# A hybrid decoder trunk on one core: the retention queries' projection ahead of the first gated-linear heads' projection

## The chip, the cores and the metric

The kernel runs on one core of a Trainium2 chip. The metric is the device time of one execution in microseconds (us). The engines that appear below are TensorE (PE, its weight load PEld), VectorE (DVE), ScalarE (ACT), GpSimd (POOL) and SyncE (SP, which issues the DMAs). Each runs its own instruction stream in order, and waits on semaphores of the others.

## The reference

There are two layers. Each is a half-step SwiGLU feed-forward block (FFN), a parallel mixing of tokens by three groups of heads, and a second half-step FFN; a final RMSNorm ends the trunk. There are 512 tokens, the model is 1024 wide and the FFN 2816, all in float32.

```python
for l in range(DEPTH):
    h = rms_norm(x, ffn1_norm[l])
    x = x + 0.5 * swiglu_ffn(h, ffn1_w_gate[l], ffn1_w_up[l], ffn1_w_down[l])
    h = rms_norm(x, mix_norm[l])
    (a_q, a_f, a_i, a_g, b_q, b_k, b_v, b_z, b_beta, b_a,
     c_q, c_k, c_v, c_g) = jnp.split(h @ w_in[l], SPLIT_IDX, axis=-1)
    o_a = hgrn2_mixer(a_q, a_f, a_i, a_g, lbs[l], hgrn_norm[l])
    o_b = gated_deltanet_mixer(b_q, b_k, b_v, b_z, b_beta, b_a, ...)
    o_c = retention_mixer(c_q, c_k, c_v, c_g, positions)
    mixed = jnp.concatenate([o_a, o_b, o_c], axis=-1)
    x = x + mixed @ w_out[l]
    h = rms_norm(x, ffn2_norm[l])
    x = x + 0.5 * swiglu_ffn(h, ffn2_w_gate[l], ffn2_w_up[l], ffn2_w_down[l])
return rms_norm(x, final_norm)
```

Each mixer has four heads. Group a is gated linear attention (HGRN2) with a decay per feature. Group b is the gated delta rule, which convolves q, k and v, and in each chunk of tokens solves a unit lower triangular system before it scans over the chunks. Group c is retention, which rotates q and k by the token's position (rope) and has a fixed decay per head.

## The kernel before, in words

**Dense products.** Every float32 operand of a dense product is split in two float32r parts, `hi` (a rounding on ScalarE) and `lo` (the remainder, on VectorE, or on GpSimd for every second split of a mixer: `POOL_LO`, `split`, line 199). A product is three matmuls. The FFNs are dense products alone (`mm3`, recorded as line 217).

**The mixer** (`mix`, line 1231) runs two things against each other. `dense_stream` (line 278) yields the matmuls of the input projection one at a time, in the order of `PLAN` (line 115), and then those of the output projection. The chains are Python generators that issue the work of the heads in steps. `interleave` (line 1308) takes a step of a chain when the chain is due by an estimate of the engines' time, and dense matmuls otherwise. A chain's step has a scheduling priority (`PRIO`: 4000 for b, 3000 for a and c, 500 for `pre`), and a limited number of chains runs at once (`LIMIT`, `CHAINS`).

A name in `PLAN` stands for one or more units of the input projection:

- `t0`: the retention values and the small gates of b. Tokens are on the partitions ("tm").
- `b0`, `b1`: q, k and v of the delta-rule heads 0, 1 and 2, 3. Features are on the partitions ("fm"); each of the three units has 256 columns, and each 128 of them are 24 matmuls of 512 columns. When a block is done, `b_conv` convolves it (tile `braw`), and after the last v `b_start` (line 599) and two `b_chain` (line 688) follow.
- `a0`, `a1`: f and q of the gated-linear heads 0, 1 and 2, 3, in "fm". `a_chain` (line 871) and `a_head` (line 912) follow.
- `ai`: the gated-linear values, in "tm".
- `cq`, `ck`: the retention queries and keys, in "tm", 256 columns: 96 matmuls of 256 columns. `c_rope` (line 1103) rotates each (tiles `craw`, `ctmp`, `crot`); when both are rotated two `c_pair` (line 1138) are queued (tiles `ps_kv`, `ps_cs`, `ps_co`).
- `bz0`, `bz1`, `cg`, `ag`: the output gates.

The triangular systems of a pair of b heads are inverted in `b_blocks` (line 638), a chain of small VectorE operations on the tiles `blk_s`, `blk_p`, `blk_x` and `inv`. The decays inside a chunk of a gated-linear head are built in levels: `aw` on VectorE, `ps_al` on TensorE, `a` back on VectorE. A `b_chain` ends in a scan over four chunks (`ps_scan`).

When all heads of a group and its gates are done, `out_group` normalises and gates it, and `flip_out` transposes and splits it (tiles `ps_mt`, `mh`, `ml`). The output projection adds the groups in three parts, `OUT_PARTS`: b0 with c, then b1, then a (matmuls `ps_out`). A part of `dense_stream` waits for its groups in this order, and the last part is in `out_proj`.

**Loads.** `stream_units` (line 230) walks the same plan. It issues one DMA of 1024 KB per 256 columns of an "fm" unit and two of 512 KB per "tm" unit on SP's queue, into two `raw` buffers, and each split goes to one of four `hi` and four `lo` buffers; `fetch` asks for the next while a unit is being multiplied.

Of the kernel before, what the change touches and what calls it, by code (L numbers as in the profile page):

```python
# [111 lines left out]
GROUP = {"a": 0, "b0": 1, "b1": 2, "c": 3}  # L112

OUT_PARTS = (('b0', 'c'), ('b1',), ('a',))
PLAN = 't0 b0 a0 ai cq b1 ck bz0 cg a1 ag bz1'

LIMIT = {'b': 4, 'a': 2, 'c': 2, 'pre': 9}
CHAINS = 6
# [47 lines left out]
class Kern:  # L166
# [1064 lines left out]
    def mix(self, l):  # L1231
# [12 lines left out]
        with self.pool(name="lay", bufs=1) as self.lay:  # L1244
# [54 lines left out]
            }  # L1299
            plan = [u for name in PLAN.split() for u in parts[name]]  # L1300
            self.units = self.stream_units(plan, self.io["w_out"][l])
# [223 lines left out]
```

## Time and profile before

| What | Value |
|---|---|
| Median of three runs | 2191.91 us (2185.59 to 2193.06) |
| Profiled execution | 2192.0 us, its span 2190.2 us |
| Mixer of layer 0, with the ends beside it | 375.6 to 753.4 us of the span |
| Mixer of layer 1, with the ends beside it | 1457.0 to 1834.2 us |
| Mean granted clock of TensorE | 0.992 |
| Bytes moved by DMA | 203.08 MB, mean 93 GB/s |

The span is the time between the first and the last instruction of the profile. A matmul's busy time overlaps that of the next one: one of 512 columns is shown with 0.39 us, while two of them start 0.23 us apart, so the distance between the starts is what one costs. The granted clock is 1.00 at full speed. A helper records most operations at one line (149 for VectorE, ScalarE and GpSimd, 260 and 265 for TensorE in the mixer), so groups are told apart by their tiles.

### The profile page before, as it was taken

How to read it: one execution, taken by the hardware profiler on the slowest of the kernel's cores; microseconds unless marked ns; L12 is line 12 of the kernel's file. 1: busy time of each engine (PE TensorE's matmuls, PEld its weight loads, DVE VectorE, ACT ScalarE, POOL GpSimd, SP SyncE). 2: the span in 40 equal slices, each digit the busy share in tenths (PEclk: the TensorE clock that was granted, in tenths of full speed). 3: DMA queues.
4: the chain of work that ended last, by engine and by line, in shares of the span. 5: the costliest groups of instructions: out<-in, count | busy, mean ns of one | idle time of the engine just before them, and what ended most of it. 6: DMA issues, size and time to landing. Idle time of an engine off the chain costs nothing.

```text
span 2190.2 us, 31776 instructions
## 1 busy us (share of the span) xinstructions
PE 2154.9 (98%) x13079; PEld 1829.6 (84%) x13079; DVE 1147.9 (52%) x1980; ACT 842.4 (38%) x1319; POOL 500.4 (23%) x466
## 2 busy tenths in 40 slices
PE   8999999998999999999999999999899999999998
PEld 7888888887988788888888888888889888888888
DVE  5544345468497743433543343364866876434335
ACT  5322224555555422222432222254654544222225
POOL 2201013454333210101211010133633412101011
PEclk9999999999999999999999999999999999999999
DMA  4323234221123323232232322242121232323223
GB/s 155 126 78 116 77 106 140 73 78 40 59 60 106 97 97 96 78 115 80 94 116 96 97 97 96 82 148 79 59 59 40 73 103 88 104 94 99 96 87 126
DMA packets 197757, 203.08 MB, mean 93 GB/s; under 512 B 7626, under 2 KB 189292, under 8 KB 197612
## 3 DMA queue, kind: packets, MB, share of 16 engines
q1 hardware_dynamic: 197612, 201.05, 29.0%
q8 instruction: 103, 1.69, 0.3%
q14 instruction: 42, 0.34, 0.0%
HBM read 194.74 MB, written 6.29 MB: 92 GB/s over the span
## 4 chain that ended last, share of the span: by engine, by line
PE 86%; DVE 9%; ACT 2%; issue 1%; POOL 0%; DMA 0%; SPq 0%; DVEq 0%; ACTq 0%; POOLq 0%
PE pd L217 22%; PE pu L217 22%; PE pg L217 22%; PE ps_fm L260 7%; PE ps_tm L260 5%; PE ps_out L260 2%; DVE aw L149 1%; PE ps_scan L265 1%; DVE lo L149 1%; PE ps_ss L265 1%; DVE blk_p L149 1%; DVE x L149 1%; PE ps_ao L265 1%; DVE flo L149 1%; PE ps_al L265 0%
## 5 line engine op out<-in xcount | busy, mean ns | idle before, releaser
L149 ACT CAST hi<-raw 128x1024 fp32r<-128x1024 f32 (+2 forms) x369 | 379.2, 1028 | 1094.2 <-PE pg L217 323.0
L149 DVE TENSOR_TENSOR lo<-raw,hi 128x1024 fp32r<-128x1024 f32 (+2 forms) x325 | 390.2, 1201 | 80.9 <-ACT hi L149 68.5
L149 POOL TENSOR_TENSOR g<-g,rstd 128x512 f32<-128x512 f32 x88 | 150.2, 1706 | 1130.2 <-ACT g L146 1130.2
L217 PE MATMUL pd<-ah,hi 128*128 128x512 f32 (+1 forms) x752 | 282.0, 375 | 0.0
L217 PE MATMUL pd<-ah,lo 128*128 128x512 f32 (+1 forms) x752 | 281.6, 375 | 0.0
L217 PE MATMUL pd<-al,hi 128*128 128x512 f32 (+1 forms) x752 | 281.6, 375 | 0.0
L217 PE MATMUL pg<-xl,hi 128*128 128x512 f32 x704 | 275.0, 391 | 1.0 <-DVE xl L149 1.0
L217 PE MATMUL pu<-xh,hi 128*128 128x512 f32 x704 | 274.4, 390 | 0.6 <-ACT hi L149 0.6
L217 PE MATMUL pg<-xh,hi 128*128 128x512 f32 x704 | 274.5, 390 | 0.1
L217 PE MATMUL pg<-xh,lo 128*128 128x512 f32 x704 | 274.2, 389 | 0.0
L217 PE MATMUL pu<-xh,lo 128*128 128x512 f32 x704 | 274.1, 389 | 0.0
L217 PE MATMUL pu<-xl,hi 128*128 128x512 f32 x704 | 273.9, 389 | 0.0
L149 DVE TENSOR_TENSOR u<-pu,g 128x512 f32<-128x512 f32 x88 | 60.9, 692 | 280.7 <-PE pu L217 265.2
L149 DVE SCALAR_TENSOR_TENSOR x<-pd,x 128x512 f32<-128x512 f32 (+1 forms) x104 | 67.4, 649 | 229.3 <-PE pd L217 229.0
L149 DVE TENSOR_TENSOR g<-pg,rstd 128x512 f32<-128x512 f32 x88 | 60.8, 691 | 206.8 <-PE pg L217 206.7
L217 PEld LDWEIGHTS pd<-al,hi 128*128 128x128 f32 x752 | 141.4, 188 | 25.7
L217 PEld LDWEIGHTS pd<-ah,lo 128*128 128x128 f32 x752 | 141.3, 188 | 25.4
L217 PEld LDWEIGHTS pd<-ah,hi 128*128 128x128 f32 x752 | 141.1, 188 | 25.5
L217 PEld LDWEIGHTS pg<-xl,hi 128*128 128x128 f32 x704 | 132.3, 188 | 29.3 <-DVE xl L149 2.1
L217 PEld LDWEIGHTS pg<-xh,hi 128*128 128x128 f32 x704 | 132.5, 188 | 27.8 <-ACT xh L149 0.4
L217 PEld LDWEIGHTS pu<-xh,hi 128*128 128x128 f32 x704 | 132.1, 188 | 28.2 <-ACT hi L149 1.0
L217 PEld LDWEIGHTS pu<-xh,lo 128*128 128x128 f32 x704 | 132.3, 188 | 27.5
(331 smaller groups left out, 3778.5 us busy)
## 6 DMA issues: line engine op xcount, KB each, us to landing
raw<-in_ffn_w_gate_dram SPq DMA_DIRECT2D x43, 1024.0 KB, 5.1
raw<-in_ffn_w_up_dram SPq DMA_DIRECT2D x43, 1024.0 KB, 5.1
raw<-in_ffn_w_down_dram SPq DMA_DIRECT2D x32, 1024.0 KB, 4.7
raw<-in_w_in_dram SPq DMA_DIRECT2D x20, 1024.0 KB, 5.2
raw<-in_w_in_dram SPq DMA_DIRECT2D x32, 512.0 KB, 3.6
raw<-in_ffn_w_down_dram SPq DMA_DIRECT2D x20, 768.0 KB, 4.4
xd<-x SPq DMA_DIRECT2D x16, 256.0 KB, 2.5
raw<-in_w_out_dram SPq DMA_DIRECT2D x16, 256.0 KB, 2.6
```

Of the source, the lines that this page charges most:

```text
L149: return f(*args, **kw)
L217: self.nc.tensor.matmul(ps, a[:, k, :], b, start=n == 0, stop=n == 3 * nk - 1)
L260: self.nc.tensor.matmul(ps, a, b, start=start, stop=stop)
L265: self.nc.tensor.matmul(ps, a, b, start=start, stop=stop)
```

## The change

The order of the units in `PLAN` changes. Nothing else does.

```diff
 OUT_PARTS = (('b0', 'c'), ('b1',), ('a',))
-PLAN = 't0 b0 a0 ai cq b1 ck bz0 cg a1 ag bz1'
+PLAN = 't0 b0 cq a0 ai ck b1 bz0 cg a1 ag bz1'
```

Two units move: `cq` from behind `ai` to ahead of `a0`, and `ck` from behind `b1` to ahead of it. So `a0` and `ai` have one more unit ahead of them, `b1` has one more, and from `bz0` on the same units stand in the same places. The loads and splits of the weights follow the same order. The chains are queued when their units are done, so their steps move with the units.

## The prediction

> **What bounds the kernel now.** I read the page first: the span, the engines and the weight loads of the mixers (count, KB each, us to landing).
>
> ```profile
> span 2190.2 us, 31776 instructions
> PE 2154.9 (98%) x13079; PEld 1829.6 (84%) x13079; DVE 1147.9 (52%) x1980; ACT 842.4 (38%) x1319; POOL 500.4 (23%) x466
> raw<-in_w_in_dram SPq DMA_DIRECT2D x20, 1024.0 KB, 5.2
> raw<-in_w_in_dram SPq DMA_DIRECT2D x32, 512.0 KB, 3.6
> ```
>
> TensorE is busy 98% of the span. An order of products removes none of them, so all that it can win is time in which TensorE idles or runs slowly, and all that it can lose is new time of that kind. The next view is the busy time by stretches: span of the stretch, then PE, PEld, DVE, ACT and POOL busy with instruction counts, then TensorE's granted clock, DMA share and GB/s. The first two rows are the mixers of layer 0 and 1 with their ends; the others are 15 us pieces.
>
> ```profile
> 375.60:753.40 377.80, 366.55 (x3316) 322.67 (x3315) 265.23 (x601) 200.12 (x375) 149.46 (x169) 0.98 0.24 72
> 1457.00:1834.20 377.20, 365.57 (x3316) 323.24 (x3315) 264.15 (x599) 201.01 (x375) 148.27 (x166) 0.98 0.24 73
> ...
> 480.00:495.00 15.00, 12.58 (x110) 9.92 (x109) 14.52 (x31) 7.67 (x12) 12.76 (x22) 0.89 0.13 36
> 495.00:510.00 15.00, 11.85 (x170) 9.49 (x169) 15.00 (x34) 6.17 (x16) 6.68 (x8) 0.89 0.13 36
> 510.00:525.00 15.00, 12.49 (x234) 9.54 (x235) 14.47 (x31) 6.42 (x9) 7.76 (x9) 0.89 0.13 37
> 660.00:675.00 15.00, 13.84 (x267) 12.33 (x266) 12.67 (x35) 10.78 (x25) 7.33 (x13) 1.00 0.45 135
> 675.00:690.00 15.00, 14.77 (x228) 12.34 (x227) 10.23 (x22) 8.21 (x21) 4.42 (x5) 1.00 0.32 115
> 1560.00:1575.00 15.00, 12.57 (x110) 10.03 (x110) 14.52 (x31) 7.80 (x12) 12.76 (x22) 0.89 0.12 35
> 1575.00:1590.00 15.00, 11.49 (x169) 9.39 (x168) 15.00 (x34) 6.16 (x16) 6.59 (x8) 0.89 0.14 38
> 1590.00:1605.00 15.00, 11.97 (x320) 9.76 (x318) 14.93 (x34) 6.42 (x10) 6.84 (x13) 0.95 0.14 37
> ```
>
> Each mixer leaves 377.80 - 366.55 = 11.2 and 377.20 - 365.57 = 11.6 us idle, and most of it sits in one place. In 480 to 525 TensorE is busy 36.9 of 45 us (8.1 idle), and the clock of 0.89 takes another 3 x 0.11 x 15 = 4.95: 13.0 us. In layer 1 the same 45 us have 9.0 idle and 4.0 of slow clock: 13.0 again. VectorE is full there (14.5, 15.0, 14.5 of 15). So **this stretch is bound by VectorE, and the rest of the mixer by TensorE**. The waits of TensorE in layer 0, and rows of the timeline of TensorE and of VectorE, say on what it waits (start, duration, engine, operation):
>
> ```profile
> PE ps_al L265 <- DVE a L149: 3.1, 1, 3.1
> PE ps_al L265 <- DVE ak L149: 2.4, 2, 2.1
> PE ps_fm L260 <- issue: 1.7, 1, 1.7
> ```
>
> ```profile
> 490.95 0.63 PE L260 MATMUL ps_fm<-xl,hi 128*128 128x512 f32 x1
> 517.92 0.73 PE L260 MATMUL ps_fm<-xh,hi 128*128 128x512 f32 x1 [1.70 <-issue]
> ```
>
> ```profile
> 466.94 1.58 DVE L149 TENSOR_TENSOR blk_s<-mt,cst 128x512 f32<-128x512 f32 x1
> 514.81 1.62 DVE L149 TENSOR_TENSOR inv<-blk_t,cst 128x128 f32<-128x128 f32 x2
> 516.69 1.21 DVE L149 TENSOR_TENSOR lo<-raw,hi 128x1024 fp32r<-128x1024 f32 x1
> 545.10 0.69 DVE L149 TENSOR_TENSOR braw<-ps_fm,rstd 128x512 f32<-128x512 f32 x1 [1.82 <-PE ps_fm L260]
> 593.84 0.91 DVE L149 TENSOR_TENSOR blk_s<-mt,cst 128x512 f32<-128x512 f32 x1
> 622.23 0.68 DVE L149 TENSOR_TENSOR inv<-blk_t,cst 128x128 f32<-128x128 f32 x2
> 706.17 1.40 DVE L149 SCALAR_TENSOR_TENSOR ml<-ps_mt,sv_a,mh 128x512 fp32r<-128x512 f32 x2
> 716.66 3.21 DVE L149 SCALAR_TENSOR_TENSOR o_a<-o_a,hr,g_a 128x64 f32<-128x64 f32 x16
> ```
>
> Three things queue on VectorE at once: the block inverses of the first delta-rule heads (b0: 466.94 to 516.4, 49.5 us, where b1's take 593.84 to 622.9, 29 us), the products of the first gated-linear heads (a0: the ps_al waits, in 480 to 525), and the rotation of the retention queries (cq). Even the dense stream waits: the weight remainder `lo` ends at 517.90 and TensorE starts at 517.92, the wait that the page calls issue.
>
> **The change part by part.** The dense order becomes t0, b0, cq, a0, ai, ck, b1, and from bz0 on it is as before. So cq stands ahead of a0 and ai, and ck ahead of b1, which the change's name doesn't say. The price of such a unit, by the chain of waits:
>
> ```profile
> 381.22 6.65 PE ps_tm L260 x54
> 398.46 19.73 PE ps_fm L260 x86
> ```
>
> 6.65 / 54 = 0.123 us per matmul, 96 of them: 11.8 us (a 512 wide product, second row, is 19.73 / 86 = 0.229). Then a0 comes 11.8 us later than now, b1 comes 11.8 us later, and ck earlier by all of b1's products and what lies between them. The loads move with their units on SP's queue: a unit of this kind brings two of 512 KB at 3.6 us each in 11.8 us of products, a feature unit one of 1024 KB at 5.2 us for 48 x 0.229 = 11.0; the DMA share stays below one half, so I put their cost at nothing. If that cover failed it would be some 5 us a layer, one landing.
>
> *VectorE's queue between 465 and 525.* cq's rotation leaves it (first row: what touches ctmp, DVE busy then POOL), and ck's comes in, from 560 to 585 (second row):
>
> ```profile
> 480.00:520.00 40.00, 5.28 (x8) 3.28 (x4) 0.89 0.12 31
> 560.00:585.00 25.00, 6.07 (x8) 2.59 (x3) 0.93 0.21 66
> ```
>
> That is an even exchange. What changes is a0: its work arrives 11.8 us later, so b0's inverses have VectorE nearly to themselves at first. If they run like b1's (29 us) they end near 496, where now they end at 516, and a0's levels, now in 480 to 525, come after them. Bounds for what is left of the 13.0 us: nothing better than the second gated-linear heads, which run the same levels without inverses beside them (660 to 690: 1.16 + 0.23 = 1.4 us idle, clock 1.00), and nothing worse than 13.0, as the same VectorE work then lies over a time 11.8 us longer. I take **5.0**: nearer the first, because the inverses go, and not at it, because ck's rotation stays beside a0. The gain is G = 8.0 us per layer.
>
> *b1's end.* b1's last convolution input is read at 545.10 and its mixed rows are ready at 706.17 + 1.40 = 707.6: 162.5 us, in steps. The end of the mixer is the next row (first product of the FFN), and the two output parts ahead of it, b1's and a's, are 96 products of 0.229 us, 22.0 us:
>
> ```profile
> 734.27 0.39 PE L217 MATMUL pg<-xh,hi 128*128 128x512 f32 x1
> ```
>
> So b1's part starts at 712.3 at the latest, 4.7 us after it is ready; a's transposes and waits come off that, and I take 2 us of slack (bounds 0 and 4.7). Group a's rows are done at 716.66 + 3.21 = 719.9, and its 48 products must start by 734.3 - 11.0 = 723.3. Both ends are nearly tight now. After the change b1's dense end moves by ck's 11.8, plus what else is pulled ahead of it, less G. Pulled ahead are the retention pairs, whose products take (ps_kv, ps_cs, ps_co in this order, PE first; DVE is the third figure):
>
> ```profile
> 560.00:612.00 52.00, 1.66 (x12) 1.50 (x12) 0.67 (x2) 0.63 (x2) 0.97 0.14 43
> 560.00:612.00 52.00, 3.50 (x32) 3.30 (x32) 2.54 (x4) 0.97 0.14 43
> 560.00:612.00 52.00, 5.23 (x44) 5.16 (x44) 1.41 (x4) 0.97 0.14 43
> ```
>
> Together 10.4 us. Now ck's unit can't end before 545.1 + 11.8 = 557, and the pairs lie between there and 612, at most 55 us behind. After the change it ends near 480 + 11.8 = 492, so the pairs come by 547, ahead of b1's end. An earlier b0 can also bring part of its scan ahead (first row below, up to 7.96 us from 545 to 570). Bounds: 11.8 - 8.0 = +3.8 with nothing pulled ahead, 11.8 + 10.4 + 8.0 - 8.0 = +22.2 with all. I take **+14.2**, the pairs alone. From there b1's steps lose company on VectorE: ck's rotation (6.07) and the pairs (0.67 + 2.54 + 1.41), 10.7 us. Bounds 0 and 10.7; I take all, as they are the whole difference in company there. b1 is ready 3.5 us later than now, while TensorE is at its part 8.0 earlier: a wait of 3.5 - 2 + 8.0 = 9.5 us. While TensorE has nothing else the steps of the scan need not share it:
>
> ```profile
> 545.00:570.00 25.00, 7.96 (x46) 6.33 (x46) 3.00 (x9) 3.66 (x10) 0.98 0.36 107
> ...
> 650.00:692.00 42.00, 11.24 (x68) 9.31 (x68) 3.62 (x12) 5.16 (x15) 1.00 0.36 115
> ```
>
> b1's scan has 11.24 + 3.62 + 5.16 = 20 us of work in 42 us, so half of the wait closes up: 4.8 us stays. Such a stop costs a slow stretch of clock as those at 480 to 525 did, 0.11 x 15 = 1.65 us. Behind the waiting product on TensorE stand a's part and the FFN, so all of it counts. Given back: 4.8 + 1.6 = 6.4 us.
>
> Trainium skill, "TensorE: Matmul & The Clock Gate", Part 1: a free-running window of about 3.4 us with too little activity halves the clock until a busy window has passed. By that figure a stop costs an estimated 1.7 us; the matmuls of 0.63 us in the first of the three pieces agree. It speaks against the change, which makes a long wait at the end out of several short ones.
>
> **Sum.** Per layer -8.0 + 6.4 = -1.6, twice: -3.2 us. The profiled execution took 2192.0 us (span 2190.2 and 1.8 around), the median of the three runs is 2191.91, so no correction: **2188.8 us**. A measurement of this kernel tells 0.3%, 6.6 us, from no change.
>
> **The rivals.** *Faster: b1 isn't late* (chance 0.35). If the pairs fall behind b1's end, b1's dense end moves by 3.8, it is ready 6.9 us earlier, and no wait arises: -8.0 per layer, 2176.0. For it: ck's rotation has to pass a VectorE that is full up to 525; against it: priority 3000 puts pairs ahead of dense products. With the stall down to 1.4 it would be 2 x 11.6, 2168.8.
>
> *Slower: b1 is later still* (0.17). With the whole +22.2 and no shortening the wait is 22.2 - 2 + 8.0 = 28.2, half of it 14.1, with 1.65: +7.8 per layer, 2207.5. One mechanism: b1's mixed rows are the last to arrive at the output product. It decides from a wait of 2 x (8.0 - 1.65) = 12.7 us, b1 ready 6.7 us later than now.
>
> *The stall stays* (0.11). These rows show VectorE blocked beside GpSimd:
>
> ```profile
> 497.33 0.41 DVE L149 TENSOR_TENSOR aw<-ae,aq 128x256 f32<-128x256 f32 x1
> 497.67 2.61 DVE L149 TENSOR_TENSOR aw<-ae,ak 128x256 f32<-128x256 f32 x1
> ```
>
> ```profile
> 497.50 2.49 POOL L149 TENSOR_TENSOR lo<-raw,hi 128x1024 fp32r<-128x1024 f32 x1 [0.37 <-ACT hi L149]
> ```
>
> An operation of 0.41 takes 2.61 us until GpSimd's `lo` ends at 499.99. Every second split is GpSimd's in the new order as well, so this part of the stall can't leave. If all stays: G = 0, b1's end moves by 22.2, it is ready 11.5 later, the wait is 9.5, given back 6.4 per layer: 2204.8. The Trainium skill, "SBUF — State Buffer", section "SBUF: two separate sides", has the rule: the port pair of the two engines is locked for a whole instruction, and the other blocks fully. The trace agrees.
>
> **How the numbers follow.** Forecast 0.37 (own range 2182 to 2196), the others 0.35, 0.17, 0.11. Leaving out a tenth at each side gives 2172 to 2208. Faster by over 0.3%: 0.35 and 0.03 of the forecast's lower edge, 0.38; within: 0.34; slower: 0.17 + 0.11, 0.28.
>
> **What would show it.** In the windows at 480 to 540 PE idle near 3 us and clock near 0.95 show G right; b0's `inv` near 496 shows why; a `ps_out` that waits some 5 us for b1's `ml` near 700 shows the price. G is wrong if ps_al still waits 3 us for `a`; the end is wrong if the last wait is for group a. All of it fails if the scheduler places chains and dense products in another way than I carry over from this trace.

## The result, and the profile after

The changed kernel takes **2254.94 us** (median of six runs, 2245.61 to 2255.93) against 2191.17 us (six runs of the kernel before beside it): 1.029 times as long, 95% interval 1.0268 to 1.0311. The forecast was 2188.8 us in a range of 2172 to 2208, so the time lies 47 us above its upper end. The profiled execution took 2255.93 us, 63.9 us more than that of before. Two executions among all runs below, one of e16 and one of the kernel before beside e5 to e7, took over 4330 us and are left out of every median.

The page of the changed kernel, its span and its engines:

```profile
span 2254.1 us, 31843 instructions
PE 2191.8 (97%) x13079; PEld 1854.3 (82%) x13079; DVE 1150.9 (51%) x1980; ACT 848.0 (38%) x1323; POOL 498.6 (22%) x466
```

The same 13079 matmuls are busy 36.9 us longer (2191.8 against 2154.9), and TensorE is idle 27.0 us longer (62.3 against 35.3). So more than half of the loss shows as matmuls that take longer, that is as granted clock (0.974 in the mean, 0.992 before), and only the rest as waiting. Where both happen is seen in the windows of the changed kernel (span of the stretch, PE, PEld, DVE, ACT and POOL busy with counts, granted clock, DMA share, GB/s):

```profile
480.00:495.00 15.00, 15.00 (x120) 14.37 (x118) 14.69 (x33) 10.73 (x17) 5.76 (x7) 1.00 0.24 71
495.00:510.00 15.00, 9.62 (x277) 7.80 (x277) 14.58 (x25) 4.61 (x8) 15.00 (x23) 0.89 0.13 37
510.00:525.00 15.00, 13.16 (x257) 10.79 (x257) 13.69 (x41) 9.21 (x25) 7.08 (x18) 0.77 0.01 2
...
645.00:660.00 15.00, 13.16 (x157) 12.82 (x157) 14.86 (x27) 7.53 (x13) 6.11 (x8) 0.89 0.22 71
660.00:675.00 15.00, 12.63 (x206) 10.47 (x205) 5.68 (x15) 9.84 (x18) 9.62 (x18) 0.77 0.46 160
675.00:690.00 15.00, 15.00 (x188) 11.90 (x187) 8.02 (x18) 6.33 (x11) 5.33 (x8) 1.00 0.31 98
690.00:705.00 15.00, 10.69 (x234) 8.53 (x232) 14.00 (x33) 5.42 (x12) 7.05 (x7) 0.98 0.32 98
705.00:720.00 15.00, 14.93 (x91) 13.34 (x91) 3.92 (x17) 5.21 (x17) 1.14 (x4) 0.50 0.22 72
720.00:735.00 15.00, 12.57 (x69) 10.57 (x68) 9.26 (x41) 6.17 (x16) 0.00 (x0) 0.83 0.00 0
735.00:750.00 15.00, 9.39 (x28) 7.04 (x29) 8.07 (x27) 3.17 (x7) 0.00 (x0) 0.54 0.01 2
```

and in those of the kernel before that the prediction had not shown:

```profile
645.00:660.00 15.00, 14.66 (x132) 14.33 (x131) 12.10 (x18) 10.58 (x20) 8.10 (x12) 1.00 0.22 70
...
690.00:705.00 15.00, 15.00 (x96) 13.13 (x95) 11.71 (x34) 5.08 (x11) 2.39 (x1) 1.00 0.14 40
705.00:720.00 15.00, 14.38 (x71) 11.73 (x70) 13.41 (x39) 4.76 (x8) 2.39 (x1) 1.00 0.42 138
720.00:735.00 15.00, 14.65 (x65) 11.20 (x64) 14.17 (x18) 10.04 (x16) 4.86 (x4) 1.00 0.00 0
```

Counted as in the prediction (idle time, and for each window 15 us times what the clock lacks of 1.00), the mixer of layer 0 divides like this. "Before" ends at 734.3, "after" at 770.1.

| Stretch of layer 0 | Before: idle + clock | After: idle + clock | Difference |
|---|---|---|---|
| 480 to 525 | 8.1 + 4.95 = 13.0 | 7.2 + 5.1 = 12.3 | -0.7 |
| 645 to 690 | 1.7 + 0 = 1.7 | 4.2 + 5.1 = 9.3 | +7.6 |
| 690 to 750 (before: to the end) | 1.0 + 0 = 1.0 | 12.4 + 17.25 = 29.7 | +28.7 |
| the other windows | 3.5 | 4.6 | +1.1 |
| all | 19.2 | 55.9 | +36.7 |

The mixer's end moved from 734.27 to 770.10, 35.8 us, so these windows hold the whole loss of the layer; the mixer of layer 1 takes 29.4 us longer (387.7 against 358.3). The count prices a low clock also where TensorE only waits, so how a row divides into idle time and clock is bookkeeping. Two things are to be read: the stall at 480 to 525, which was to shrink, is still there, and there is a new hole in 690 to 750. TensorE's timeline of the changed kernel shows the hole from both sides (start, duration, engine, line, operation, and in brackets the wait ahead of it):

```profile
564.84 0.39 PE L260 MATMUL ps_fm<-xh,lo 128*128 128x512 f32 x1
...
698.17 0.39 PE L260 MATMUL ps_out<-mh,lo 128*128 128x512 f32 x1
705.88 0.80 PE L265 MATMUL ps_scan<-bv_tm,bxt 128*128 128x128 f32 x2
...
744.14 1.65 PE L260 MATMUL ps_out<-mh,hi 128*128 128x512 f32 x3 [0.51 <-ACT mh L149]
...
770.10 0.47 PE L217 MATMUL pg<-xh,hi 128*128 128x512 f32 x1 [0.17 <-DVE x L149]
```

The first output part is through at 698.5 (the prediction looked for its wait near 700), the next output product comes at 744.1. For 46 us, 43 in layer 1, the dense stream stands and waits for b1, and only the small matmuls of b1's scan and of the second gated-linear heads are left. Below, this hole is called **the stop**. VectorE's rows give b1's way there:

```profile
577.05 0.69 DVE L149 TENSOR_TENSOR braw<-ps_fm,rstd 128x512 f32<-128x512 f32 x1
...
619.06 0.68 DVE L149 TENSOR_TENSOR blk_s<-mt,cst 128x512 f32<-128x512 f32 x1
657.75 0.66 DVE L149 TENSOR_TENSOR inv<-blk_t,cst 128x128 f32<-128x128 f32 x2
...
734.59 1.41 DVE L149 SCALAR_TENSOR_TENSOR ml<-ps_mt,sv_a,mh 128x512 fp32r<-128x512 f32 x2 [0.49 <-ACT mh L149]
744.12 1.41 DVE L149 SCALAR_TENSOR_TENSOR ml<-ps_mt,sv_a,mh 128x512 fp32r<-128x512 f32 x2 [1.02 <-ACT mh L149]
```

The `ml` at 734.59 is group a's, the one at 744.12 is b1's: b1 is now last of all, ready at 745.5 where it was 707.6. Two rows of TensorE in the kernel before complete the comparison, the last product of b1's projection and the first of its scan:

```profile
544.67 0.40 PE L260 MATMUL ps_fm<-xh,lo 128*128 128x512 f32 x1
651.31 0.46 PE L265 MATMUL ps_scan<-bv_tm,bxt 128*128 128x128 f32 x2
```

| Step of b1, layer 0, us | Before | After |
|---|---|---|
| last product of its projection starts, us of the span | 544.7 | 564.8 |
| until its last convolution input is read | 0.4 | 12.2 |
| until `blk_s` | 48.7 | 42.0 |
| inverses, `blk_s` to the end of `inv` | 29.1 | 39.4 |
| until the first product of its scan | 28.4 | 47.5 |
| until its mixed rows are ready | 56.3 | 39.6 |
| from the projection to the rows | 162.9 | 180.7 |

b1's input is 20.2 us late, and its way is 17.8 us longer on top. Of these, 11.8 us come before the last convolution input is read. That read is VectorE's, but VectorE isn't full when the input is there. It is busy 4.93 of the 11.98 us; its rows ahead of the read wait for products of b0's scan and of the retention pairs, the longest 5.1 us for `ps_scan` (the window from the end of the projection's products to the read, in the same columns as above):

```profile
565.07:577.05 11.98, 11.98 (x101) 11.48 (x100) 4.93 (x12) 3.60 (x7) 3.62 (x2) 1.00 0.29 88
```

### The profile page after: what moved, and what is told of

Same layout as the page of the kernel before. It is cut to its first block, busy times and chain, and to the rows that moved or that the text cites. A ratio compares the mean times of both kernels' runs of the same rounds, so it can differ in the third digit from the quotient of the medians.

```text
span 2254.1 us, 31843 instructions
## 1 busy us (share of the span) xinstructions
PE 2191.8 (97%) x13079; PEld 1854.3 (82%) x13079; DVE 1150.9 (51%) x1980; ACT 848.0 (38%) x1323; POOL 498.6 (22%) x466
## 4 chain that ended last, share of the span: by engine, by line
PE 88%; DVE 8%; issue 1%; ACT 1%; POOL 1%; DMA 0%; SPq 0%; DVEq 0%
PE pd L217 21%; PE pu L217 21%; PE pg L217 21%; PE ps_fm L260 7%; PE ps_tm L260 5%; PE ps_out L260 4%; PE ps_scan L265 1%; DVE blk_p L149 1%; DVE aw L149 1%; PE ps_ao L265 1%; PE ps_ss L265 1%; DVE af L149 1%; PE ps_al L265 1%; DVE lo L149 1%; DVE flo L149 1%
## 5 line engine op out<-in xcount | busy, mean ns | idle before, releaser
L217 PEld LDWEIGHTS pu<-xh,lo 128*128 128x128 f32 x704 | 132.1, 188 | 28.4 <-DVE lo L149 0.8
L217 PEld LDWEIGHTS pg<-xh,lo 128*128 128x128 f32 x704 | 132.4, 188 | 27.3
```

The costliest lines, as they stand in the source:

```text
L217: self.nc.tensor.matmul(ps, a[:, k, :], b, start=n == 0, stop=n == 3 * nk - 1)
```

## The experiments

All times are medians beside runs of the kernel before on the same chip (2188.7 to 2190.6 us from e1 on). "b1" is the start of the transposing products of b1's rows and "stop" the longest time from one output product to the next, start to start, both in layer 0, b1 counted from the mixer's first dense product; the end is that of the mixer of layer 0 on the same clock.

| Run | us | Ratio, 95% interval | b1 projection read | b1 | Stop | End |
|---|---|---|---|---|---|---|
| before | 2191.2 | 1 | 169.7 | 328.8 | 4.6 | 358.8 |
| after | 2254.9 | 1.029 [1.0268, 1.0311] | 200.9 | 365.2 | 46.0 | 394.0 |
| e1 cq alone | 2221.1 | 1.0134 [1.0119, 1.015] | 166.9 | 340.5 | 12.1 | 369.2 |
| e2 ck alone | 2247.5 | 1.0257 [1.024, 1.0274] | 193.3 | 356.4 | 38.7 | 385.5 |
| e3 a's part first | 2246.8 | 1.0249 [1.0228, 1.027] | 200.9 | 370.2 | 32.6 | 385.4 |
| e4 gate in ck's place | 2236.2 | 1.0205 [1.0188, 1.0222] | 184.2 | 351.4 | 25.0 | 379.7 |
| e5 b1 ahead of cq | 2224.5 | 1.0167 [1.0151, 1.0183] | 149.4 | 330.2 | 8.5 | 373.7 |
| e6 b1 behind cq | 2234.9 | 1.0216 [1.02, 1.0232] | 108.7 | 340.2 | 8.9 | 381.3 |
| e7 after, all due soon | 2251.5 | 1.0292 [1.0275, 1.031] | 213.0 | 358.6 | 26.0 | 385.5 |
| e7 before, all due soon | 2255.8 | 1.0301 [1.0276, 1.0326] | 188.3 | 351.9 | 7.9 | 390.7 |
| e8 inverses first | 2252.6 | 1.0291 [1.0276, 1.0306] | 201.9 | 362.5 | 41.7 | 391.1 |
| e9 filled stop | 2273.9 | 1.0394 [1.0378, 1.0409] | 205.7 | 377.3 | 52.7 | 406.0 |
| e10 after, no GpSimd remainders | 2238.0 | 1.0223 [1.0208, 1.0238] | 191.9 | 359.8 | 45.5 | 388.1 |
| e11 a1 ahead of a gate | 2214.3 | 1.0113 [1.0096, 1.013] | 166.9 | 335.4 | 5.4 | 369.3 |
| e12 after, b1 due at once | 2224.3 | 1.0152 [1.0137, 1.0168] | 200.6 | 337.4 | 7.2 | 374.9 |
| e13 before, b1 due at once | 2235.2 | 1.0204 [1.0187, 1.0221] | 166.9 | 325.9 | 10.5 | 377.1 |
| e14 after, b1 and a1 at once | 2220.0 | 1.013 [1.0115, 1.0145] | 202.0 | 347.9 | 16.8 | 374.8 |
| e15 before, b1 and a1 at once | 2230.0 | 1.0177 [1.0162, 1.0192] | 168.5 | 341.3 | 8.3 | 380.0 |
| e16 e14 and e10 together | 2206.9 | 1.0078 [1.0058, 1.0097] | 190.3 | 336.5 | 18.1 | 363.5 |
| e17 before, no GpSimd remainders | 2200.0 | 1.0042 [1.0026, 1.0058] | 154.4 | 329.4 | 2.8 | 359.9 |

### Which of the two moved units: e1, e2, e4

```diff
 # after:         PLAN = 't0 b0 cq a0 ai ck b1 bz0 cg a1 ag bz1'
+# e1_cq_alone
+PLAN = 't0 b0 cq a0 ai b1 ck bz0 cg a1 ag bz1'
+# e2_ck_alone
+PLAN = 't0 b0 a0 ai cq ck b1 bz0 cg a1 ag bz1'
+# e4_gate_for_ck
+PLAN = 't0 b0 a0 ai cq bz0 b1 ck cg a1 ag bz1'
```

> Only cq moves, from behind ai to ahead of a0; ck stays behind b1, so b1 has the same units ahead of it as before the change. Theory (b1 comes too late because ck is ahead of it, and its output part stops TensorE): within 10 us of the 2191 of before, b1's last mixed rows within 5 us of 707.6 in layer 0. Rival (a0, 11.8 us later, crowds the second half): most of the loss stays, 2230 or more.

> Only ck moves, from behind b1 to ahead of it; cq stays behind ai. Theory (b1 too late): most of the loss of the change, 2235 to 2260, with no output product between about 698 and 740 in layer 0. Rival (a0 late): within 10 us of 2191.

> The order of before, with bz0 (a gate's unit of the same 96 matmuls, with no chain of its own) moved ahead of b1, and ck left behind b1. If it is the 11.8 us of dense products ahead of b1 that make it late: 2225 to 2260, like ck alone. If it is the retention pairs, which are pulled ahead of b1's end only by ck: less than half of the loss, under 2215.

ck ahead of b1, alone, makes a stop of 38.7 us and 57 us of the 64 that are lost; cq ahead of a0, alone, makes a stop of 12.1 us and costs 31, between the two expectations of e1. They don't add. With b's first output gate in ck's place, b1 again has a unit more ahead of it, and the stop is 25.0 us. So **the long stop comes with a unit ahead of b1**, whichever it is, and with ck it is longer than with the gate: b1's projection is read 23.6 us later than before in e2, 14.5 in e4.

e1 also tests the stall beside the first gated-linear heads, since there ck's rotation isn't near it. Its windows:

```profile
495.00:510.00 15.00, 8.83 (x250) 7.40 (x254) 14.96 (x25) 4.27 (x6) 12.11 (x19) 0.92 0.12 37
510.00:525.00 15.00, 10.70 (x159) 8.21 (x151) 14.96 (x32) 8.25 (x17) 6.13 (x8) 0.84 0.15 43
525.00:540.00 15.00, 13.54 (x264) 11.37 (x265) 8.78 (x24) 8.84 (x26) 7.06 (x15) 0.67 0.22 67
```

Idle 6.2 + 4.3 + 1.5 and clock 1.2 + 2.4 + 4.95 make 20.5 us, more than in either kernel. The keys' rotation alone isn't what keeps the stall: without it VectorE is as full (14.96 of 15), as b1's convolutions have come into its place (`bk`, `bq` and `braw`, 3.3 + 2.9 + 2.0 = 8.2 us in 495 to 525 by the groups of this run).

### The parts' order, the inverses' rank, and the clock: e3, e8, e9

```diff
+# e3_a_part_first
-OUT_PARTS = (('b0', 'c'), ('b1',), ('a',))
+OUT_PARTS = (('b0', 'c'), ('a',), ('b1',))
+# e8_blocks_first: b_blocks in a queue of its own
-PRIO = {'b': 4000, 'a': 3000, 'c': 3000, 'pre': 500}
+PRIO = {'b': 4000, 'a': 3000, 'c': 3000, 'blk': 4000, 'pre': 500}
+# e9_fill, in the loop in which an output part waits for its groups
+self.room(1)
+ps = self.pa.tile([P, T], F32, tag="a", name="ps_fill")
+for k in range(4):
+    self.nc.tensor.matmul(ps, self.xs[k][0][:, 0:P], self.xs[k][0], start=k == 0, stop=k == 3)
```

> The changed order, with the output part of group a ahead of that of b1. After the change a's mixed rows are ready at 736.0 and b1's at 745.5 in layer 0. Theory (TensorE stops for b1 alone): a's 48 products, 11 us, run in b1's wait, 8 to 11 us less per layer, 2233 to 2239. Rival (both groups end together, because TensorE itself is the bound there): 2255 as after the change, within 5.

> The changed order, with the block inverses at the priority of the delta-rule chains (4000 for 500). In the changed kernel b1's inverses take 39.4 us, against 29.1 before the change, in a stretch where VectorE is full. If it is the queue on VectorE that makes b1 late: 30 us for them, 8 to 10 us less of the stop per layer, 2235 to 2240. If the builder's due times decide, or VectorE's load as such: within 6 of 2255.

> The changed order, with four extra 512 wide products into an unread tile at each pass of the wait for b1 (they add work and change no output). In the stop of the changed kernel the granted clock is 0.68. If the slow clock is a good part of the loss: the clock there goes to 0.9 or more and the mixer ends 4 to 12 us earlier per layer, 2231 to 2247. If the chain's own latency is all: the fillers stand in its way, 2255 to 2275.

Group a's part ahead of b1's uses some of the stop (32.6 instead of 46.0 us) and wins 8 us in all, where its theory had 8 to 11 in each layer: a's rows are only 10 us earlier than b1's, and with a's part in front b1's transposes come 5.0 us later than in the changed kernel. The inverses in a queue of the delta rule's own rank still take 39.3 us, and nothing changes: what stretches them isn't the rank of their steps.

e9 adds products that nothing reads, to hold the clock up while the dense stream waits. The stop in its windows, and below it that of the changed kernel:

```profile
703.00:755.70 52.70, 46.23 (x412) 38.85 (x410) 26.93 (x92) 16.25 (x45) 5.01 (x6) 0.95 0.09 28
```

```profile
698.50:744.10 45.60, 33.22 (x307) 28.23 (x306) 26.20 (x91) 16.46 (x45) 4.62 (x5) 0.68 0.09 31
```

The clock rises from 0.68 to 0.95, and still the stop gets 6.7 us longer (52.7 against 46.0, start to start). The low clock accompanies the stop, but to buy it back with 104 more products in line costs more than it brings. What the clock alone costs there this doesn't show, as the fillers themselves stand in the chain's way. That leaves b1's own chain as what has to be shortened.

### b1 earlier in the order: e5, e6, e11

```diff
+# e5_b1_up_one
+PLAN = 't0 b0 a0 ai b1 cq ck bz0 cg a1 ag bz1'
+# e6_b1_behind_cq
+PLAN = 't0 b0 cq b1 a0 ai ck bz0 cg a1 ag bz1'
+# e11_a1_up (the order of before, a1 ahead of cg)
+PLAN = 't0 b0 a0 ai cq b1 ck bz0 a1 cg ag bz1'
```

> The order of before with b1 one unit earlier, ahead of cq. Theory (b1's readiness decides the end of the mixer, and before the change it had about 2 us of slack, with group a as tight): b1's last mixed rows some 8 to 12 us earlier, the end set by group a, 2180 to 2195. Rival (what costs is any step away from the order of before, through crowding on VectorE): 2210 or more.

> The changed order with b1 alone taken forward, to right behind cq; cq still stands between b0 and a0. Theory (the loss is b1's lateness at the output projection): the stop at b1's part is gone, but a0 is now later by b1's 33 us; 2180 to 2210. Rival (cq ahead of a0 costs by itself, by a0 being late): 2220 or more.

> The order of before with a1 one unit earlier, ahead of cg. Before the change the mixer's end is set by group a, with b1 some 2 us behind, and the first output part waits for nothing. If there is anything to gain in the order: a is ready up to 10 us earlier, b1 then decides, 2182 to 2191. If b1's chain is crowded by it, as in the runs so far: 2200 to 2230.

These three say most on carrying a chain's length from one order to another. In e5 b1's projection is read 20 us earlier than in the kernel before, and b1's transposes come 1.4 us *later*; in e6 it is read 61 us earlier, and they come 11.4 us later. So **the length of b1's way isn't its own**: from the projection to the transposes it is 159.1 us before, 164.3 after, 180.8 in e5 and 231.5 in e6. All three orders are slower than before. In e5 and e6 the longest wait of TensorE in the mixer is the transposing product's for `o_a` (4.6 and 4.9 us): group a is late instead of b1.

### When the builder takes b1's steps: e7, e12 to e15

`interleave` gives a chain's next step a due time: an estimate of when its input is there, stretched by `LAT`, and `STEP` ns more. What is left open by the runs so far is whether b1's steps are spaced out by these due times or by the load of VectorE beside them.

```diff
+# e7_after_soon, e7_before_soon: for all chains
-STEP = 1600
+STEP = 800
...
-LAT = 1.4
+LAT = 1.0
+# e12 (after), e13 (before): SOON = ('b1',);  e14 (after), e15 (before): SOON = ('b1', 'a1')
+soon = self.late(r[2]) in SOON
...
-r[0] = max(self.done * LAT + self.pe * (1 - LAT), self.pe) + STEP
+lat, step = (1.0, 800) if soon else (LAT, STEP)
+r[0] = max(self.done * lat + self.pe * (1 - lat), self.pe) + step
```

`late` names the group of a chain: those of heads 2 and 3 and the output group that goes with them (group a's has all four heads).

> The changed order, with the chains' steps handed out sooner by the builder (STEP 800 for 1600, LAT 1.0 for 1.4). If b1's chain is late because its steps are spaced by the builder, and not by the engines: the stop of 46 us shrinks to half or less, 2225 or less. If the engines set it (VectorE full at 615 to 660): within 15 of 2255.

> The order of before with the same sooner steps. It has hardly a stop to close, and steps handed out too soon make TensorE wait: 2190 to 2215 in either theory. It shows what the two constants do by themselves.

> The changed kernel; only the steps of the second delta-rule heads (b1: start, two chains, inverses, output group) are now due as soon as the builder's estimate has their input, where each was due an estimated spacing later. Theory A (b1 is late because the builder spaces its steps out): b1's inverses, 39 us in the changed kernel, come back to about 30, the merges behind them close up, b1's rows are ready 20 to 30 us earlier, the stop of 46 and 43 us ahead of b1's output part shrinks to 15 to 25, time 2205 to 2235. Rival B (the engines are loaded, and the spacing only mirrors it): the steps then wait on VectorE instead, the stop stays above 35 us, time 2245 to 2262.

> The same edit of b1's due times on the kernel before. There b1 is ready only some 2 to 5 us ahead of its output part, so there is next to nothing for it to win: theory A expects b1's rows ready 10 to 20 us earlier at about the same time, 2185 to 2205. Rival B: PE is held by b1's products in the middle of the dense stream (they were spaced to avoid it), 2205 to 2240.

> The changed kernel with b1's and the second gated-linear heads' (a1, with its output group) steps due as soon as the estimate has their input. Theory A: as with b1 alone, and a1 isn't pushed back by it: stop of 15 to 25 us, 2205 to 2235. Rival B: b1 and a1 compete for VectorE as before, the stop stays above 35 us, 2245 to 2262.

> The kernel before with the same edit of b1's and a1's due times. Theory A: both groups are ready earlier, nothing on the path to win but the last few us of a: 2183 to 2200. Rival B: more stops in the middle of the dense stream, 2205 to 2245, as with all chains due soon (2255.8).

With the due times of all chains cut, both kernels take about the same (2251 and 2256 us): the stop shrinks to 26.0 us after, and in the kernel before other waits arise, 29.4 us of idle time in layer 0 instead of 10.7. By its expectation e7 speaks for the engines (within 15 of 2255), but with the chains all pulled forward at once. With b1's alone, **e12 wins 30.7 us of the 63.8**, inside what theory A gave. Its VectorE rows for b1, and the first product of b1's scan (the line numbers of these runs are one higher):

```profile
576.63 0.69 DVE L150 TENSOR_TENSOR braw<-ps_fm,rstd 128x512 f32<-128x512 f32 x1
...
611.50 1.61 DVE L150 TENSOR_TENSOR blk_s<-mt,cst 128x512 f32<-128x512 f32 x1
...
645.53 0.66 DVE L150 TENSOR_TENSOR inv<-blk_t,cst 128x128 f32<-128x128 f32 x2
...
716.49 0.74 DVE L150 SCALAR_TENSOR_TENSOR ml<-ps_mt,sv_a,mh 128x512 fp32r<-128x512 f32 x1
```

```profile
664.48 0.63 PE L266 MATMUL ps_scan<-bv_tm,bxt 128*128 128x128 f32 x2
```

The projection is read at the same time as after (576.6 against 577.1). From there `blk_s` takes 34.9 us (42.0 after), the inverses 34.7 (39.4), the way to the scan 18.3 (47.5), the scan to the rows 52.8 (39.6): 140.6 us instead of 168.5. The largest part, 29 us, is between the inverses and the scan. The stop is 7.2 us in layer 0 (15.7 in layer 1). Rival B, in which the engines' load sets the pace, needed a stop above 35 us and falls for this part; the inverses, which close up by only 4.7 us where theory A had about 9, leave it a share. VectorE's load in the two stretches agrees (`blk_s` to the end of `inv` before and after, then the way to the scan after):

```profile
593.84:622.91 29.07, 29.07 (x202) 26.64 (x201) 26.43 (x74) 13.15 (x23) 8.22 (x15) 1.00 0.14 37
```

```profile
619.06:658.41 39.35, 37.51 (x307) 34.06 (x306) 38.80 (x111) 19.59 (x29) 13.46 (x10) 0.98 0.29 89
658.41:705.88 47.47, 40.72 (x637) 32.97 (x635) 30.10 (x69) 21.59 (x41) 22.52 (x33) 0.90 0.35 114
```

During the inverses VectorE is now busy 38.8 of 39.35 us. The inverses' own operations take as much of it as before (14.7 against 14.6 us); what is new beside them are the first operations of a1 (`af`, `flo`, `aq`, `ak`: 8.9 us, where it was 0.6) and those of the output groups of b0 and c (`hv`, `hr`, `rs_t`, `o_b`, `o_c`, `ml`: 11.8, where it was 4.6). On the way to the scan VectorE is busy only 30.1 of 47.5 us, and that way is what the due times close.

Then a is the next to be late (its transposes at 357.7), which e14 changes a little.

The same edit makes the kernel **before** slower, by 45 us for b1 and 40 for both, as the rivals of e13 and e15 had it: TensorE idles 27.4 us in layer 0 of e13, where it was 10.7. Nor does it shorten b1's way there, from the projection to the transposes 159.0 us against 159.1: what these due times hold up in the changed order, they don't in this one. With b1 due at once the changed order is the faster of the two (2224.3 against 2235.2). So neither the order nor the due times are good or bad alone.

### GpSimd's remainders: e10, e16, e17

```diff
-POOL_LO = range(2, 70, 2)
+POOL_LO = ()
```

> The changed order, with no weight remainder on GpSimd (all of them on VectorE). If the stall at 495 to 520 stayed because VectorE is blocked beside GpSimd's remainders: TensorE's idle and slow time there falls from 12 to 8 us or less per layer. Against it VectorE gets some 1.2 us for each of 19 splits per layer, in its full stretches too: 2245 to 2270.

> The changed kernel with b1's and a1's steps due at once, and every weight remainder on VectorE (none on GpSimd). Theory: the change's loss has two parts that add, the late steps of b1 (won back in part by the due times) and the stall beside the first gated-linear heads, to which GpSimd's remainders contribute. Taking them off VectorE's port gave 17 us in the changed kernel, so 2203 to 2212 here, 495 to 520 with a clock above 0.9. Rival: VectorE is so full beside b1 and a1 that 32 more remainders on it cost what the lock gave: 2218 to 2230.

> The kernel before with every weight remainder on VectorE. If GpSimd's remainders lengthen the stall of 480 to 525 there as they do in the changed kernel, 3 to 6 us a layer come back and nothing is late at the end: 2178 to 2185, a version ahead of both. Rival: that stall is VectorE's own work (15.0 of 15 us busy), to which the remainders only add: 2192 to 2205.

In e10's windows the stall is less than half of what it was:

```profile
495.00:510.00 15.00, 11.98 (x347) 9.56 (x347) 14.97 (x30) 5.72 (x13) 10.27 (x20) 0.89 0.13 38
510.00:525.00 15.00, 14.65 (x296) 12.05 (x295) 14.83 (x37) 10.44 (x25) 11.57 (x17) 1.00 0.12 38
```

Idle 3.0 + 0.35 and clock 1.65, with none in 480 to 495, are 5.0 us: 7.3 less than after, and e10 is 16.9 us faster over two layers, 7 us below the range that it was given. That edit isn't free, though. In the kernel before it costs 9.4 us (e17, the rival of its expectation), so it gives no version ahead of both. The stall of 480 to 525 shrinks there too, but only by 2.2 us: 7.4 idle and 3.45 of clock are 10.8, and VectorE stays full. With the due times it adds up: 2254.9, less 35.0 for b1's and a1's due times, less 13.1 here, is e16's 2206.9. **That leaves 16.3 us above the kernel before**, and none of the versions tried beats it.

## Why the prediction was wrong

**b0's inverses** were right. They were to end near 496 after some 29 us; they end at 499.5, after 32.4 us (VectorE of the changed kernel):

```profile
467.12 0.69 DVE L149 TENSOR_TENSOR blk_s<-mt,cst 128x512 f32<-128x512 f32 x1
...
498.82 0.68 DVE L149 TENSOR_TENSOR inv<-blk_t,cst 128x128 f32<-128x128 f32 x2
```

**G, the stall that shrinks from 13.0 to 5.0, failed**: 12.3 us are left, G is 0.7. Two steps failed in it. One is the choice of the nearest row, "the inverses go", so that the first gated-linear heads would run nearly like the second ones. The windows of the tile `aw` alone (PE, PEld, DVE, then clock) say why. First the kernel before, then the changed one:

```profile
495.00:510.00 15.00, 1.31 (x128) 1.21 (x128) 9.19 (x16) 0.89 0.13 36
510.00:525.00 15.00, 1.54 (x128) 1.35 (x128) 1.61 (x4) 0.89 0.13 37
```

```profile
495.00:510.00 15.00, 2.23 (x128) 1.83 (x128) 4.56 (x8) 0.89 0.13 37
510.00:525.00 15.00, 1.82 (x128) 1.61 (x128) 5.81 (x12) 0.77 0.01 2
```

The levels come at 495 to 525 in both, 20 operations and 10.8 and 10.4 us of VectorE, though their products are one unit later. Before, they lay on the last 20 us of the inverses; now they come right behind them, and the room that the inverses left is taken by ck's rotation, which stands where cq's stood. e1, with b1's convolutions in that room, has the same full VectorE. So VectorE stays full without the inverses, by whatever the next unit brings. The second gated-linear heads have no such unit, and so were no measure for the first; no run has the first ones with nothing beside them. The other step is GpSimd's remainder, which the prediction showed in its own rows under "The stall stays" and left out of the forecast. One operation of each engine, and the wait of TensorE behind them:

```profile
500.20 2.36 POOL L149 TENSOR_TENSOR lo<-raw,hi 128x1024 fp32r<-128x1024 f32 x1
500.28 2.57 DVE L149 TENSOR_TENSOR crot<-ctmp 128x256 f32<-128x256 f32 x1 [0.39 <-POOL ctmp L149]
...
504.03 0.31 PE L265 MATMUL ps_al<-aw 128*32 128x16 f32 x12 [2.20 <-DVE aw L149]
```

The rotation's step ends at 502.85, 0.29 us after `lo`, where a step of that shape takes 0.42 us in most other places. The rule of the Trainium skill that the prediction cites ("SBUF — State Buffer", section "SBUF: two separate sides") agrees with this row, and e10 prices it in this order: 7.3 of the 12.3 us go when the remainders leave GpSimd. The 5.0 that stay, with ck's rotation beside the levels, are the forecast's own number. "The stall stays" had 0.11.

**b1's dense end** was to move by 14.2 us, bounds 3.8 and 22.2. It moved by 20.2. By the prediction's own sum with G as measured it would be 11.8 + 10.4 - 0.7 = 21.5, which is near, but in part by luck: of the pairs' products all 44 of `ps_co` (5.2 of the 10.4 us) come only behind b1's last product, and 20 products of b0's scan, which the forecast had left out, come ahead of it. What the sum put at nothing is the read of the last convolution input. The pairs and b0's scan, still under way on TensorE, hold up VectorE's rows ahead of it, and it comes 11.8 us later still: 32.0 us later than before, where 14.2 was forecast.

**b1's chain, 10.7 us shorter**, failed as much. Counted from that read as in the prediction, it got 6.0 us longer (168.5 against 162.5). The prediction subtracted the company that b1 loses on VectorE, the rotation and the pairs, and called this the whole difference. But b1's inverses now run beside a1's first operations and two output groups, and the way from them to the scan is held up by the due times of b1's steps: e12 takes back 28 us by those alone. e5 and e6 show that the length of the chain can't be carried over at all. The prediction named this as what could fail ("the scheduler places chains and dense products in another way than I carry over"), and gave it no chance. Together the two steps, 17.8 and 16.7 us, make b1 ready 38.0 us later, where 3.5 was forecast.

**The wait** was put at 9.5 us, of which half would close up, and 1.65 us of clock. It is 46 us. The closing up is real and larger than forecast: the scan to the rows takes 39.6 us instead of 56.3. The clock's price was mis-sized most: 17.25 us in 690 to 750 against 1.65, since the clock is at half for 20.5 and for 13.8 us there and not for one short stretch. What of it lengthened the stop isn't shown: the scan ran its 39.6 us at half the clock for the most part.

Per layer the forecast was -1.6. G is short by 7.3; the stop costs 28.7 where 6.4 was given back, 22.3 more; 645 to 690 adds 7.6, where b1's stretched inverses meet a1; together 35.6, and 35.8 was measured. So two of the rivals came true at once, "the stall stays" and "b1 is later still". The latter decides from b1 ready 6.7 us later, and it was 38.0 later; its stop was priced at 14.1 + 1.65 = 15.75 us and cost 28.7. The two had been priced as alternatives, and the range ended where either of them ended alone.

**What stays open**: the 16.3 us that e16 is above the kernel before, why the due times space out b1's steps in the changed order and not in the old one, and what the low clock costs by itself.

## What to carry to other kernels

When chains are placed by a planner, their length is a property of the plan and not of the chain: before carrying a duration over to another order, ask what sets the distance of its steps, and what new company the chain gets where it lands. A group that is ready only a few us before it is needed has no slack to give, so a unit put ahead of it costs its own length and whatever the planner then does with the rest, here with the clock at half for most of it. A stall on a full engine doesn't go when one of its tenants goes, if the next unit's work moves in, or if another engine's operations block it.

## What the hardware showed unexpectedly

A busy TensorE didn't mean a high clock. In 705 to 720 its matmul records fill 14.93 of 15 us and the granted clock is 0.50, and none of the waits in the stop is long (TensorE's waits in 690 to 745: us in total, times, longest):

```profile
PE ps_mt L271 <- DVE o_b L149: 4.6, 1, 4.6
PE ps_ak L271 <- DVE ak L149: 2.6, 1, 2.6
PE ps_a L265 <- DVE ak L149: 1.7, 1, 1.7
```

The wait of 4.6 us is the last one, ahead of 741.3, long after the clock had first dropped, at 704.5; the waits of 1.7 and 2.6 us end at 701.5 and 705.1. The windows cut at the changes of the clock:

```profile
704.50:725.00 20.50, 19.93 (x114) 18.34 (x115) 4.79 (x19) 7.27 (x23) 1.14 (x4) 0.50 0.16 52
725.00:735.20 10.20, 7.57 (x46) 5.57 (x45) 9.09 (x39) 4.31 (x12) 0.00 (x0) 1.00 0.00 0
735.20:749.00 13.80, 8.39 (x24) 6.22 (x25) 7.73 (x26) 2.97 (x6) 0.00 (x0) 0.51 0.01 2
```

The Trainium skill, "TensorE: Matmul & The Clock Gate", Part 1, has the clock back at full speed after one window of about 3.4 us of sustained activity. Here small matmuls in sequence left it at half for 20.5 us, with records on 19.9 of them. It then came back while still only small matmuls ran, and with 512-wide products among them (e9) it stood at 0.95. What the chip counts as activity no run here shows; that matmul records on nearly all of 20 us didn't bring it back sooner, this trace does.
